# The start of a two-block network kernel: loads of parameters, input and first weights in another order, first column blocks by token halves

## The chip, the cores and the metric

The kernel runs on one core of one Trainium2 chip. The metric is the device time of one execution, in microseconds; the median of the runs counts.

## What is computed

The reference is two blocks of a sequence model on one sequence of 1024 tokens with 1024 features in float32. The first has an RWKV-7 branch and a differential attention, both fed from one projection, then a mixture of 32 experts and a gated embedding; the second has three recurrent mixers (SSD, HGRN, S5). What matters here is how the first one begins:

```python
h = rms_norm(x, norm_mix[l])
proj = h @ w_in[l]
p_rwkv = proj[..., :RWKV_COLS]
...
def rwkv7_branch(pr, mu, w0, ...):
    prev = jnp.pad(pr[:, :-1], ((0, 0), (1, 0), (0, 0)))
    xs = pr + (prev - pr) * mu
```

Every projected column of the RWKV branch (1792 of them) is mixed with the token before by a factor mu of its own.

## The kernel before

The kernel is written with a planner: the program says in its order which tiles are made from which, and the planner sets the order of the instructions on each engine and in each queue from its own estimate of times, the program's order being the preference among what is ready. Tiles live in pools; a pool that is closed gives its space to the next one on its side, and an instruction that writes the new tile waits until the old tile in that space has been used.

The input x has eight token tiles of 128 x 1024. norm_in (L2110) loads the gain of the norm on all partitions, then for each tile: the load (three buffers), in norm_tile (L183) the sum of squares on ScalarE (L189), a small operation on VectorE (L190), a power on GpSimd (L177), and the scaled tile on VectorE (L192). transpose_split (L195) then has TensorE transpose it in two batches of four (L202), ScalarE write the rounded part hi to hT (L205) and VectorE the rest lo (L206).

rwkv_proj (L290) goes through 14 blocks of 128 columns in the order RWKV_ORDER. load_w (L208) loads a block's weights of 1024 x 128 through one buffer and splits them in hi (ScalarE, L181) and lo (VectorE, L182), which have two buffers each. gemm_fm makes a block's product for 512 tokens, half the sequence, from eight groups of three products (L262 to L264), 24 in all, into one of two PSUM tiles "mm"; ScalarE (L303) and VectorE (L304) mix it with the token before, and the last token of the first half is kept in "edge" (L309). Both halves of a block are done before the next block. L303 and L304 need the parameters: setup_params (L149) loads 15 small arrays as rows of one tile "prows" (L156), TensorE transposes it (L159) and VectorE copies it to pcol (L160).

branches (L2133) calls norm_in, setup_params, rwkv_proj, then rope_tables (L626; tables for the attention's rotation, loaded, multiplied by the gains and stored) and rwkv_core (L325), which first stores zeros to two scratch arrays (L331 to L337), loads constants, and then works through eight units of the recurrence. Behind it come the attention's projections, the gates' (16 blocks) and the attention. All these loads and most stores are issued by SyncE's queue.

Of the kernel before, what the change touches and what calls it, by code (L numbers as in the profile page):

```python
# [11 lines left out]
F32 = mybir.dt.float32  # L12
F32R = mybir.dt.float32r
I32 = mybir.dt.int32
# [8 lines left out]
T = 1024  # L23
D = 1024
# [4 lines left out]
def make_consts():  # L29
    """Constants that depend on shapes alone, one column block each of a [128, n] array."""  # L30
# [57 lines left out]
def flat(ap):  # L88
    """A contiguous DRAM array as one axis."""
    n = 1  # L90
    for s in ap.shape:
        n *= s
    return bass.AP(tensor=ap.tensor, offset=ap.offset, ap=[[1, n]])
# [6 lines left out]
class Parts:  # L100
    """A weight matrix split in hi + lo, in tiles of `part` blocks of 128 rows."""
# [9 lines left out]
class Kern:  # L111
# [19 lines left out]
    def const(self, *names, pool=None):  # L131
        """Load constants to SBUF tiles."""
# [15 lines left out]
    def setup_params(self):  # L148
        nc = self.nc  # L149
        with self.pool(name="prow", bufs=1) as pool:  # L150
# [3 lines left out]
            for nme, c in PARAM_ROWS:  # L154
                self.pat[nme] = o
                nc.sync.dma_start(rows[o:o + c, :], flat(self.ap[nme]).rearrange("(r c) -> r c", c=128))  # L156
# [9 lines left out]
    def bcast_row(self, pool, src, n, name, bufs=None):  # L166
        """A DRAM vector on every partition."""
# [3 lines left out]

    def rsqrt(self, out, v):
        """out = v ** -0.5, on [128, few]."""
# [5 lines left out]
    def split(self, hi, lo, src):  # L179
        """src as the sum of two float32r parts."""  # L180
# [3 lines left out]
    def norm_tile(self, pool, x, gain, out=None):  # L184
        """rms_norm of a token tile [128, 1024]."""
# [3 lines left out]
        nc.scalar.activation(h, x, AF.Square, accum_out=st[:, 0:1])  # L189
        nc.vector.tensor_scalar(st[:, 1:2], st[:, 0:1], 1.0 / D, EPS, op0=OP.mult, op1=OP.add)  # L190
        self.rsqrt(st[:, 2:3], st[:, 1:2])
        nc.vector.scalar_tensor_tensor(h, x, st[:, 2:3], gain, op0=OP.mult, op1=OP.mult)  # L192
        return h

    def transpose_split(self, hi, lo, h, j, nk=8, k0=0, tag="t"):  # L195
        """Token tile j [128, nk*128] -> feature-major hi / lo [128, k, tokens]."""
        nc = self.nc
        for q in range(nk // 4):
# [7 lines left out]
            nc.vector.tensor_sub(lo[d], pv, hi[d].bitcast(F32))  # L206

    def load_w(self, pool, w, segs, kt=KT, raw_bufs=1, bufs=2, part=4):  # L208
        """Weight columns [kt*128, segs] -> float32r hi, lo, in tiles of `part` row blocks."""
# [5 lines left out]
        for k0 in range(0, kt, part):  # L215
            raw = pool.tile([128, part, n], F32, name=self.name("wr"), tag="wraw", bufs=raw_bufs)
            lo = pool.tile([128, part, n], F32R, name=self.name("wl"), tag="wlo", bufs=bufs)
            o = 0
            for c0, c in segs:
                nc.sync.dma_start(raw[:, :, o:o + c], wv[:, k0:k0 + part, c0:c0 + c])  # L220
                o += c
            hi = pool.tile([128, part, n], F32R, name=self.name("wh"), tag="whi", bufs=bufs)
# [5 lines left out]
    def resident_w(self, pool, w, k0, kt, cs, name, raw_bufs=2, gain=None, raws=None):  # L228
        """Row blocks k0..k0+kt-1 of w, columns cs -> Parts in one pair of tiles; a generator, a block at a time,
        that returns it. gain [128, kt]: a factor of every row; raws(k): a tile for the load of a block."""  # L230
# [17 lines left out]
    def finish(self, g):  # L248
        """What the generator g returns."""
# [9 lines left out]
    def mm3(self, out, a, b, first, last):  # L259
        """out += a^T b with a, b split in (hi, lo)."""  # L260
# [1998 lines left out]
```

## Time and profile before

| | us |
|---|---|
| median of three runs | 3081.0 |
| lowest, highest | 3079.27, 3085.3 |
| span of the profiled execution | 3076.1 |
| TensorE busy in it | 2897.0 |
| VectorE busy | 1965.6 |
| ScalarE busy | 1319.5 |

The span reaches from the first to the last instruction of the profiled execution; its time outside the span isn't recorded by itself, and the median of the runs is 4.9 us above the span. PE is TensorE's products, PEld its loading of weights, DVE is VectorE, ACT ScalarE, POOL GpSimd, SPq SyncE's queue of DMA issues. A busy TensorE isn't one at its full speed: its granted clock has two levels, 1.00 standing for 2.4 GHz and 0.50 for 1.2 GHz.

### The profile page before, as it was taken

Reading aid. Unit: us, or ns where it says so; the run is one execution under the profiler, and the core shown is the slowest. Engines: PE = TensorE matmul, PEld = TensorE weight load, DVE = VectorE, ACT = ScalarE, POOL = GpSimd, SP = SyncE. Lnnn points to the kernel's source line nnn. Section 1 sums busy time; section 2 is a strip of 40 time slices with the busy share of each in tenths; the row PEclk is TensorE's granted clock in tenths of the full one; section 3 lists DMA queues with packets and bytes.
Section 4 is the critical chain, followed back from the end, with each engine's and each line's share of the span. In section 5 each row is a group of like instructions: output and inputs, shape, how many; then the busy total and the mean of one; then the engine's idle time right before and its main releaser. Section 6 shows DMA issues by size and latency. Waiting matters only on the chain. (4 is left out here: it accounts for less than half of the span.)

```text
span 3076.1 us, 47278 instructions
## 1 busy us (share of the span) xinstructions
PE 2897.0 (94%) x18410; PEld 2400.8 (78%) x18410; DVE 1965.6 (64%) x3826; ACT 1319.5 (43%) x2167; POOL 231.9 (8%) x193
## 2 busy tenths in 40 slices
PE   6999999998998989889999997999999999999998
PEld 4888888775776867678777775878988999987776
DVE  4335778644454656679988786688546754548663
ACT  3222223213454222668777775444323343333341
POOL 0000111000000000012121110000000000000000
PEclk9999989997998998999999998999999999999999
DMA  5323333323114455799999995433344442137433
GB/s 162 115 89 82 102 116 107 101 65 106 62 62 144 152 187 195 247 339 378 370 347 335 319 346 212 138 105 95 102 129 128 133 133 74 55 106 232 125 124 127
DMA packets 378145, 503.30 MB, mean 164 GB/s; under 512 B 86039, under 2 KB 234422, under 8 KB 377918
## 3 DMA queue, kind: packets, MB, share of 16 engines
q1 hardware_dynamic: 347742, 458.63, 45.1%
q0 software_dynamic: 11296, 24.57, 2.2%
q10 hardware_dynamic: 18880, 17.05, 1.6%
q8 instruction: 146, 2.39, 0.3%
q14 instruction: 81, 0.66, 0.1%
HBM read 410.26 MB, written 106.68 MB: 168 GB/s over the span
## 5 line engine op out<-in xcount | busy, mean ns | idle before, releaser
L182 DVE TENSOR_TENSOR wh<-we,wh 128x1024 fp32r<-128x1024 f32 x384 | 452.8, 1220 | 72.3 <-ACT wh L181 70.3
L181 ACT ACTIVATE wh<-we 128x1024 fp32r<-128x1024 f32 x384 | 388.5, 1058 | 59.2 <-PE b L264 32.4
L262 PE MATMUL mm<-wh,hU 128*128 128x256 f32 (+1 forms) x768 | 253.3, 332 | 5.3 <-DVE z L1358 4.0
L263 PE MATMUL mm<-wl,hU 128*128 128x256 f32 (+1 forms) x768 | 251.8, 328 | 2.5 <-DVE wl L182 2.4
L264 PE MATMUL mm<-wh,hU 128*128 128x256 f32 (+1 forms) x768 | 250.0, 326 | 0.0
L264 PE MATMUL mm<-wh,hT 128*128 128x256 f32 (+1 forms) x640 | 215.1, 337 | 0.0
L262 PE MATMUL mm<-wh,hT 128*128 128x256 f32 (+1 forms) x640 | 207.0, 341 | 2.4 <-ACT ye L1060 2.3
L262 PE MATMUL mm<-hT,wh 128*128 128x512 f32 x480 | 196.5, 409 | 4.3 <-DVE edge L309 4.2
L182 DVE TENSOR_TENSOR wl<-wr,wh 128x1024 fp32r<-128x1024 f32 (+2 forms) x102 | 116.0, 1139 | 122.6 <-ACT wh L181 113.8
L264 PE MATMUL mm<-hT,wl 128*128 128x512 f32 x480 | 191.9, 400 | 0.0
L181 ACT ACTIVATE wh<-wr 128x1024 fp32r<-128x1024 f32 (+2 forms) x102 | 100.9, 992 | 211.3 <-PE mm L263 156.8
L263 PE MATMUL mm<-hT,wh 128*128 128x512 f32 x480 | 191.5, 399 | 0.0
L262 PEld LDWEIGHTS mm<-wh,hU 128*128 128x128 f32 x768 | 183.0, 239 | 9.6 <-DVE z L1358 5.0
L263 PEld LDWEIGHTS mm<-wl,hU 128*128 128x128 f32 x768 | 184.0, 240 | 5.8 <-DVE wl L182 3.5
L264 PEld LDWEIGHTS mm<-wh,hU 128*128 128x128 f32 x768 | 184.3, 240 | 1.4 <-issue 1.4
L262 PEld LDWEIGHTS mm<-wh,hT 128*128 128x128 f32 x640 | 125.0, 196 | 21.3 <-issue 4.3
L264 PEld LDWEIGHTS mm<-wh,hT 128*128 128x128 f32 x640 | 125.5, 196 | 12.6 <-issue 1.5
L262 PE MATMUL mm<-hU,wh 128*128 128x512 f32 x320 | 128.6, 402 | 4.5 <-ACT wh L181 4.5
L263 PE MATMUL mm<-hU,wh 128*128 128x512 f32 x320 | 127.3, 398 | 0.0
L264 PE MATMUL mm<-hU,wl 128*128 128x512 f32 x320 | 126.7, 396 | 0.0
L263 PE MATMUL mm<-wl,hT 128*128 128x256 f32 x384 | 115.8, 302 | 1.9 <-DVE wl L182 1.9
L262 PEld LDWEIGHTS mm<-hT,wh 128*128 128x128 f32 x480 | 92.3, 192 | 31.4 <-ACT xs L303 4.5
(704 smaller groups left out, 7098.1 us busy)
## 6 DMA issues: line engine op xcount, KB each, us to landing
we<-w_gate SPq DMA_DIRECT2D x64, 1024.0 KB
we<-w_up SPq DMA_DIRECT2D x64, 1024.0 KB
we<-w_down SPq DMA_DIRECT2D x64, 1024.0 KB
wr<-w_in SPq DMA_DIRECT2D x86, 512.0 KB
d_gate<-gz SPq DMA_DIRECT2D x32, 256.0 KB
gt<-d_gate SPq DMA_DIRECT2D x16, 512.0 KB
x<-d_x SPq DMA_DIRECT2D x16, 512.0 KB
dec<-sd_cum SPq DMA_DIRECT2D x16, 512.0 KB
```

Of the source, the lines that this page charges most:

```text
L181: self.nc.scalar.activation(hi, src, AF.Copy)
L182: self.nc.vector.tensor_sub(lo, src, hi.bitcast(F32))
L262: nc.tensor.matmul(out, a[0], b[0], start=first, stop=False)
L263: nc.tensor.matmul(out, a[0], b[1], start=False, stop=False)
L264: self.last = nc.tensor.matmul(out, a[1], b[0], start=False, stop=last)
```

## The change

Five things change; all lies in the first stage.

- setup_params is called ahead of norm_in, and its 15 loads are issued from ScalarE's queue.
- norm_in has eight buffers for x, in a pool on the other side of the memory, and issues all loads first: x tile 0, the gain, x tiles 1 to 3, the first block's weights, x tiles 4 and 5, the second block's weights, x tiles 6 and 7. The two weight tiles have buffers of their own in that pool.
- The split of the first block's weights stands behind the norm of tile 2, that of the second behind tile 4's.
- rwkv_proj does the first two blocks (12 and 13) by token halves: first half of both, then second half of both.
- rope_tables and the zeros (now rwkv_scratch) are queued behind the last x load on SyncE and behind the last split of the input on VectorE (issue_after adds an order on the same engine, without a wait between engines).

Lines that only lost a comment are left out here.

```diff
     def setup_params(self):
...
-                nc.sync.dma_start(rows[o:o + c, :], flat(self.ap[nme]).rearrange("(r c) -> r c", c=128))
+                nc.scalar.dma_start(rows[o:o + c, :], flat(self.ap[nme]).rearrange("(r c) -> r c", c=128))
...
+    @contextmanager
+    def issue_after(self, *instructions):
+        with ExitStack() as es:
+            for i in instructions:
+                es.enter_context(self.tc.issue_after(i.ins))
+            yield
...
-        nc.scalar.activation(h, x, AF.Square, accum_out=st[:, 0:1])
+        sq = nc.scalar.activation(h, x, AF.Square, accum_out=st[:, 0:1])
...
-        nc.vector.scalar_tensor_tensor(h, x, st[:, 2:3], gain, op0=OP.mult, op1=OP.mult)
+        self.normed = sq, nc.vector.scalar_tensor_tensor(h, x, st[:, 2:3], gain, op0=OP.mult, op1=OP.mult)
...
-            nc.vector.tensor_sub(lo[d], pv, hi[d].bitcast(F32))
+            self.last_split = nc.vector.tensor_sub(lo[d], pv, hi[d].bitcast(F32))
...
+    def load_w_steps(self, pool, w, segs, kt=KT, raw_bufs=1, bufs=2, part=4, raw_pool=None):
...
-            raw = pool.tile([128, part, n], F32, name=self.name("wr"), tag="wraw", bufs=raw_bufs)
+            raw = (raw_pool or pool).tile([128, part, n], F32, name=self.name("wr"), tag="wraw", bufs=raw_bufs)
...
+            yield
             hi = pool.tile([128, part, n], F32R, name=self.name("wh"), tag="whi", bufs=bufs)
...
-    for i in order:
-        w = K.load_w(wp, K.ap["w_in"][0], [(i * 128, 128)], part=KT)
-        mu = K.par("rwkv_mu", i)
-        edge = None
-        for hf in range(2):
+    ws = dict(zip(order, first_ws))
+    edges = {}
+    for group in (order[:2], *((i,) for i in order[2:])):
+        for hf, i in ((hf, i) for hf in range(2) for i in group):
+            if i not in ws:
+                ws[i] = K.load_w(wp, K.ap["w_in"][0], [(i * 128, 128)], part=KT)
+            w, mu = ws[i], K.par("rwkv_mu", i)
+            edge = edges.get(i)
...
+def rwkv_scratch(K, dp):
+    xds = []
+    with K.pool(name="rw_z", bufs=1, side="right") as zp:
+        zero = zp.tile([128, 1040], F32, name="rw_zero")
+        K.nc.vector.memset(zero, 0.0)
+        for i in range(2):
+            xd = dp.tile([2 * 16 * 4160], F32, name=f"rw_xd{i}", tag=f"xd{i}", bufs=1)
+            K.nc.sync.dma_start(dap(xd, 0, [[1040, 128], [1, 1040]]), zero)
+            xds.append(xd)
+    return xds
...
-def norm_in(K, x, gname, hT):
+def norm_in(K, x, gname, hT, first_w):
     nc = K.nc
-    with K.pool(name="ni", bufs=1) as pool:
+    with K.pool(name="ni", bufs=1, side="right") as pool:
+        xs = [pool.tile([128, D], F32, name=K.name("xt"), tag="xt", bufs=8) for _ in range(8)]
+        load = lambda j: nc.sync.dma_start(xs[j], x[j * 128:(j + 1) * 128, :])
+        first_ws = [first_w(i, pool) for i in range(2)]
+        load(0)
         gain = K.bcast_row(pool, K.ap[gname], D, "ni_gain")
+        for j in (1, 2, 3):
+            load(j)
+        next(first_ws[0])
+        for j in (4, 5):
+            load(j)
+        next(first_ws[1])
+        for j in (6, 7):
+            ld = load(j)
+        ws = []
         for j in range(8):
-            xt = pool.tile([128, D], F32, name=K.name("xt"), tag="xt", bufs=3)
-            nc.sync.dma_start(xt, x[j * 128:(j + 1) * 128, :])
-            K.transpose_split(hT[0], hT[1], K.norm_tile(pool, xt, gain), j)
+            K.transpose_split(hT[0], hT[1], K.norm_tile(pool, xs[j], gain), j)
+            if j in (2, 4):
+                with K.issue_after(*K.normed):
+                    ws.append(K.finish(first_ws[len(ws)]))
+    return (ld, K.last_split), ws
...
-            norm_in(K, x, "norm_mix", hT)
             K.setup_params()
-            rwkv_proj(K, hT, wp, xs_d, rp)
-            rope_tables(K, tab_d)
-            rwkv_core(K, xs_d, or_d)
+            first_w = lambda i, p: K.load_w_steps(wp, K.ap["w_in"][0], [(RWKV_ORDER[i] * 128, 128)], part=KT, raw_pool=p, raw_bufs=2)
+            after, ws = norm_in(K, x, "norm_mix", hT, first_w)
+            rwkv_proj(K, hT, wp, xs_d, rp, ws)
+            with K.issue_after(*after):
+                rope_tables(K, tab_d)
+                zeros = rwkv_scratch(K, dd)
+            rwkv_core(K, xs_d, or_d, zeros)
```

## Rows read from the trace of the kernel before

**Rows 1.** The page's busy time by engine, with share of span and instructions.

```profile
PE 2897.0 (94%) x18410; PEld 2400.8 (78%) x18410; DVE 1965.6 (64%) x3826; ACT 1319.5 (43%) x2167; POOL 231.9 (8%) x193
```

**Rows 2.** Busy time by stretch, columns in the first line.

```profile
core 0: us, PE busy (x) PEld busy (x) DVE busy (x) ACT busy (x) POOL busy (x), PEclk, DMA share, GB/s
0.00:58.60 58.60, 28.31 (x113) 21.27 (x114) 29.86 (x52) 23.58 (x39) 4.60 (x12) 0.96 0.51 165
58.60:200.00 141.40, 141.38 (x648) 112.88 (x649) 46.77 (x101) 34.92 (x50) 1.65 (x1) 0.98 0.35 111
200.00:700.00 500.00, 476.37 (x5716) 404.89 (x5716) 328.60 (x918) 137.43 (x250) 53.41 (x30) 0.95 0.34 96
700.00:800.00 100.00, 83.46 (x390) 55.25 (x386) 44.57 (x131) 37.94 (x106) 3.65 (x3) 0.76 0.26 86
```

**Rows 3.** TensorE's waits, 0 to 60 us: total, times, longest.

```profile
PE t L202 <- DVE hT L206: 11.7, 6, 3.7
PE t L202 <- DVE st L190: 10.5, 1, 10.5
PE mm L262 <- DVE edge L309: 4.2, 1, 4.2
PE t L202 <- DVE h L192: 4.0, 1, 4.0
```

**Rows 4.** The same for SyncE's queue.

```profile
SPq L156 <- DVE h L192: 13.7, 1, 13.7
```

**Rows 5.** Timeline of SyncE's queue, first and last of 15 loads (start, duration).

```profile
44.98 0.40 SPq L156 DMA_DIRECT2D prows<-rwkv_mu  x1
...
49.85 0.29 SPq L156 DMA_DIRECT2D prows<-norm_ple  x1
```

**Rows 6.** Groups by line, 0 to 58.6 us, VectorE: count, busy us, mean ns, idle before.

```profile
L206 DVE TENSOR_TENSOR hT<-t,hT 128x512 fp32r<-128x512 f32 x16 | 10.5, 680 | 4.3 <-ACT hT L205 4.3
L192 DVE SCALAR_TENSOR_TENSOR h<-xt,st,ni_gain 128x1024 f32<-128x1024 f32 x8 | 10.3, 1284 | 4.3 <-POOL st L177 4.3
...
L182 DVE TENSOR_TENSOR wl<-wr,wh 128x1024 fp32r<-128x1024 f32 x3 | 3.7, 1226 | 7.8 <-ACT wh L181 7.8
...
L304 DVE SCALAR_TENSOR_TENSOR xs<-mm,pcol,xs 128x511 f32<-128x511 f32 x2 | 1.5, 746 | 0.3 <-ACT xs L303 0.3
...
L190 DVE TENSOR_SCALAR st<-st 128x1 f32<-128x1 f32 x8 | 1.2, 148 | 7.8 <-ACT h L189 7.7
...
L639 DVE TENSOR_TENSOR da_tk_norm<-c_rope_sin,da_gk_norm 128x512 f32<-128x512 f32 x1 | 0.7, 691 | 2.3 <-DMA da_gk_norm<-k_norm 2.3
...
L309 DVE TENSOR_SCALAR edge<-mm,pcol 128x1 f32<-128x1 f32 x1 | 0.2, 210 | 0.0
```

**Rows 7.** Timeline of VectorE, the norms of the last two tiles.

```profile
40.24 1.28 DVE L192 SCALAR_TENSOR_TENSOR h<-xt,st,ni_gain 128x1024 f32<-128x1024 f32 x1 [0.73 <-POOL st L177]
...
43.67 1.28 DVE L192 SCALAR_TENSOR_TENSOR h<-xt,st,ni_gain 128x1024 f32<-128x1024 f32 x1 [0.73 <-POOL st L177]
```

**Rows 8.** Timeline of ScalarE and VectorE, first tile; idle before in brackets.

```profile
0.73 1.28 ACT L189 ACT_TABLE_LOAD   x1 [0.73 <-PEq L2248]
...
7.12 1.06 ACT L189 ACTIVATE h<-xt 128x1024 f32<-128x1024 f32 x1 [5.10 <-DMA xt<-x]
...
9.12 1.29 DVE L192 SCALAR_TENSOR_TENSOR h<-xt,st,ni_gain 128x1024 f32<-128x1024 f32 x1 [0.67 <-POOL st L177]
```

**Rows 9.** Timeline of TensorE: four transposes, and the product after its last wait.

```profile
37.06 0.60 PE L202 MATMUL t<-c_ident,h 128*128 128x128 f32 x4
...
58.62 0.77 PE L262 MATMUL mm<-hT,wh 128*128 128x512 f32 x1 [4.20 <-DVE edge L309]
```

**Rows 10.** Busy time by stretch, the 48 products from 58.62 us on.

```profile
58.62:63.40 4.78, 4.78 (x11) 3.77 (x12) 0.94 (x4) 1.02 (x2) 0.00 (x0) 0.50 0.90 265
63.80:71.90 8.10, 8.10 (x37) 6.57 (x35) 1.30 (x3) 1.32 (x2) 0.00 (x0) 1.00 0.28 98
```

**Rows 11.** Busy time by stretch, two stretches with loads; the last column is GB/s.

```profile
2.00:12.50 10.50, 1.97 (x8) 1.57 (x8) 2.87 (x5) 3.20 (x7) 1.10 (x2) 1.00 0.94 310
...
16.00:34.00 18.00, 8.10 (x29) 6.30 (x30) 11.94 (x19) 7.64 (x13) 2.20 (x4) 1.00 0.83 263
```

More of the change, by code (lines that the diff above doesn't have):

```diff
@@ L1 @@
 import math
-from contextlib import ExitStack
+from contextlib import ExitStack, contextmanager
 import numpy as np
@@ L205, in transpose_split, with load_w @@
             nc.scalar.activation(hi[d], pv, AF.Copy)
-            nc.vector.tensor_sub(lo[d], pv, hi[d].bitcast(F32))
-    def load_w(self, pool, w, segs, kt=KT, raw_bufs=1, bufs=2, part=4):
+            self.last_split = nc.vector.tensor_sub(lo[d], pv, hi[d].bitcast(F32))
+    def load_w(self, *a, **kw):
+        return self.finish(self.load_w_steps(*a, **kw))
+    def load_w_steps(self, pool, w, segs, kt=KT, raw_bufs=1, bufs=2, part=4, raw_pool=None):
         nc = self.nc
@@ L287, with rwkv_proj @@
 RWKV_ORDER = (12, 13, 4, 0, 8, 5, 1, 9, 6, 2, 10, 7, 3, 11)
-def rwkv_proj(K, hT, wp, xs_d, pool, order=RWKV_ORDER):
+def rwkv_proj(K, hT, wp, xs_d, pool, first_ws, order=RWKV_ORDER):
     nc = K.nc
@@ L307, in rwkv_proj @@
             else:
-                edge = pool.tile([128, 1], F32, name=K.name("edge"), tag="edge", bufs=2)
+                edge = edges[i] = pool.tile([128, 1], F32, name=K.name("edge"), tag="edge", bufs=2)
                 nc.vector.tensor_scalar(edge, p[:, 511:512], mu, None, op0=OP.mult)
@@ L319, with rwkv_core @@
         "y": 1, "st": 1, "ft": 1, "bon": 2}
-def rwkv_core(K, xs_d, o_d):
+def rwkv_scratch(K, dp):
[8 more added lines that the diff above has]
+    return xds
+def rwkv_core(K, xs_d, o_d, xds):
     HT = T // 2
@@ L329, in rwkv_core @@
     dp = es.enter_context(K.pool(name="rw_d", bufs=2, space=DRAM))
-    xds = []
-    with K.pool(name="rw_z", bufs=1) as zp:
-        zero = zp.tile([128, 1040], F32, name="rw_zero")
-        nc.vector.memset(zero, 0.0)
-        for i in range(2):
-            xd = dp.tile([2 * 16 * 4160], F32, name=f"rw_xd{i}", tag=f"xd{i}", bufs=1)
-            nc.sync.dma_start(dap(xd, 0, [[1040, 128], [1, 1040]]), zero)
-            xds.append(xd)
     late, mid, early = (es.enter_context(K.pool(name=f"rw_{n}", bufs=1)) for n in ("late", "mid", "early"))
```

## The prediction

> **What bounds the kernel now.** I read the profile from the coarse to the fine. The summary by engine says that TensorE works through 94% of the span [rows 1]. That is a mean over many stages, so the second view is the table of stretches [rows 2]: up to 58.6 us TensorE is busy for 28.31 us, idle for 30.3, and from 58.6 to 200 us it is busy for 141.38 of 141.40. So the kernel has a front of 58.6 us, in which something other than TensorE decides, and behind it a stretch without a hole, in which TensorE alone decides: whatever lets TensorE enter that stretch earlier moves all of it. Nothing later in this kernel depends on absolute time; later stages start when earlier ones end.
>
> The third view says what TensorE waits for in the front [rows 3]: 10.5 us until the first normed tile, 11.7 and 4.0 us between token tiles (VectorE's split of the tile before, and the norm), and 4.2 us, the last wait of all, until VectorE has used the parameters on two products (tile "edge"). All four together are 30.4 us, the whole idle time. Behind them stands SyncE's queue [rows 4]: it stood 13.7 us before the first parameter load, until VectorE's last norm gave the space free that the parameters' tile shares with the norm's. So the 15 parameter loads were issued from 44.98 to 50.14 us [rows 5], their transpose and copy came after the second product, and TensorE stood until 58.62 [rows 9].
>
> **The change, part by part.** I follow one state S through both kernels: all 64 transposes of the normed input done, 48 products (two half blocks) done, the next half block starting. Before, S is at 58.62 us [rows 9].
>
> *Parameters.* Their 15 loads, transpose, copy and what follows leave the end of the front; on TensorE that removes the last wait of 4.2 us, which is inside the difference of S below and isn't added to it. The loads come back at the very start on ScalarE's queue, ahead of its first activation. The 15 issues took SyncE 5.2 us from the first to the end of the last, 0.29 us for most and 0.40 for the longest [rows 5]. No row shows ScalarE issuing such loads; I take the same 5.2 us. Today ScalarE has loaded its table by 2.01 us and then stands 5.10 us until the first x tile has landed, at 7.12 [rows 8]. With the issues from 0.74 on and the table load of 1.28 us either ahead of or behind them, the first activation comes at 0.7 + 5.2 + 1.3 = 7.2 us, as now. So this costs nothing, hidden by the wait for x; without that cover it would cost 6 us. Bounds: at 0.40 us for each of the 15 it is 0.8 us later; if the table load falls within the loads' wait and the first x tile, which now goes ahead of the gain, lands one transfer earlier (0.5 MB at 310 GB/s [rows 11], 1.7 us), up to 1.7 us earlier. I take nothing, since this sum and today's row meet within 0.1 us.
> The Trainium skill (ScalarE: Activation LUTs, "What ACT_TABLE_LOAD costs") says that a load of 1283 ns is followed by a drain of some 1380 ns. The row here agrees with the first number; the second can't be seen, since ScalarE was waiting for x anyway. By it the first activation would be 1.4 us later and the gain so much smaller.
> The Trainium skill (DMA: Bandwidth & Descriptors, "Issuing engines are not separate DMA queues") also says that another issuing engine saves only the time of issuing, the transfers share the same engines. By it the move to ScalarE's queue is worth at most those 5.2 us of issue, and the rest comes from the new place of the parameters' tile. The rows say the same in another way: the 13.7 us were a wait for space.
>
> *x tiles and weights up front.* Ahead of the last x tile now stand the identity (64 KB), the gain, eight x tiles and two weight tiles, each 512 KB: 5.8 MB. The front moved 310 GB/s in its first full stretch and 263 in a later one [rows 11], which gives 19 to 22 us, so the last x tile lands at 21 to 25 us and the fourth at 11 to 13. The tables for the rotation, on whose loads VectorE stands today among its tiles (2.3 us ahead of one multiplication [rows 6]), wait behind the last x load (their loads) and behind the last split (their work on VectorE). What is late next is then VectorE's own work. A tile costs it a norm of 1.284 us, two splits of 0.680 and a small operation of 0.148 [rows 6]: 2.79 us. Two tiles that follow each other without other waits are 3.43 us apart, 40.24 to 43.67 [rows 7], because the small operation stands behind the splits and GpSimd's power behind it. A tile period of 2.79 and 3.43 are the bounds; I take the middle, 3.1, since with all x tiles there the squares can run ahead but the order isn't known. At 3.1 us a tile the loads are always ahead.
>
> *Token halves.* The first four tiles are enough for half a block. The first norm on VectorE starts at 9.1 us as today [rows 8]. Four tiles and one weight split of 1.226 us [rows 6]: 9.1 + 4 x 3.1 + 1.2 = 22.7 us. From there TensorE has 48 products and the other 32 transposes to do. The 48 products from 58.62 us on took 13.3 us, to 71.9, eleven of them at the granted clock of 0.50 and 37 at 1.00 [rows 10]; four transposes take 0.60 us in their midst [rows 9], so 32 take 4.8. So TensorE is done at 22.7 + 13.3 + 4.8 = 40.8 us. VectorE has in that time eight tiles, two weight splits, and the work behind two products, 2 x (0.746 + 0.210) = 1.9 us [rows 6]: 9.1 + 24.8 + 2.5 + 1.9 = 38.3 us. The later one decides: S at 40.8 us. With 2.79 us a tile it is 39.6, with 3.43 it is 42.1.
> Today the 11 products after S ran at a clock of 0.50, 4.78 us in place of 11 x 0.22 = 2.4, since TensorE had stood for 4.2 us. With TensorE at work without a pause up to S, this loss of 2.4 us lies before S, in the 13.3 us, and isn't paid again.
>
> *What moves behind.* Four table multiplications of 0.69 us [rows 6], the writing of the zeros, and their transfers (four stores of 0.5 MB and two constants) now fall at 40 to 50 us. VectorE is busy for 46.77 of 141.40 us there [rows 2] and the transfers have a share of 0.35, so they hide. What they feed belongs, in the program's order, behind all 14 blocks. If the cover were gone, the 4 x 0.69 = 2.8 us of VectorE would show. The third weight tile can load early in its old buffer; its split waits for the first block's second half, as today, and that leaves it a whole half block, 24 x 0.22 = 5.3 us [rows 10], for VectorE's 1.2 us [rows 6] and ScalarE's part ahead of it.
>
> *Sum.* 58.6 - 40.8 = 17.8 us, and 2.4 of clock: 20.2 us. Bounds: 58.6 - 42.1 = 16.5, without the clock and less 0.8 for the issues 15.7; 58.6 - 39.6 + 2.4 + 1.7 = 23.1. The profiled execution has a span of 3076.1 us; it would become 3056. The median of the three runs is 3081.0, 4.9 us more, which I take as lying around the span, unchanged. So 3081.0 - 20.2 gives 3061 us.
>
> **The rivals.** *Part is given back later.* The order of the instructions is made by a planner for the whole program, so another front can change the order of any later stage. A gap there has the size of 4.2 us [rows 3] up to the 16.5 us that TensorE stands idle between 700 and 800 us [rows 2]. With half of the larger one lost, 8 us, the time is 3069. For it speaks that such gaps exist in all later stages; against it, that the stages are shifted as a whole and keep their dependences. The same can close a gap: 3053.
> *It doesn't do what it says.* If the tiles keep the distance they have today on average, (43.67 - 9.12) / 7 = 4.9 us [rows 7, 8], because ScalarE's or VectorE's order puts the weights and the evacuations in badly, VectorE is done at 9.1 + 8 x 4.9 + 2.5 + 1.9 = 52.7 us and the gain is 6: 3075. Against it: at least the waits for the rotation's loads [rows 6] are gone, and VectorE's last two tiles kept 3.43.
> *Slower, the attention runs out of cover.* Between 700 and 800 us the granted clock is 0.76 and TensorE idles 16.5 us [rows 2]: there softmax decides, and TensorE fills up with gate blocks of 48 products, 10.9 us each at full clock (13.3 less 2.4). If the new order spends more than two of them ahead of the attention, in holes that were filled by other work, the attention stands without them. It decides from 26 us (two and a half blocks); three blocks cost 32.7 us, and the time is 3094. For it: TensorE is 95% busy from 200 to 700 us [rows 2], a block that moves forward fills little. Against it: the program's order of the gates isn't touched.
>
> **How the numbers follow.** The forecast (15.7 to 23.1 us less, 3058 to 3066) has a chance of 0.60; given back in part (3067 to 3077) 0.18, of which a tenth lies within 0.2%; a gap closed besides (3046 to 3057) 0.08; not done as said 0.08, within 0.2%; slower 0.06. About 0.2%, 6 us, is what a measurement of this kernel can tell from no change. Faster: 0.60 + 0.17 + 0.08 = 0.85; same 0.09; slower 0.06. For 8 in 10 the range takes the forecast, nearly all of the case given back and most of the gap closed: 3049 to 3075.
>
> **What would show it.** Right: in the profile after, TensorE's first product at 21 to 25 us; no wait of TensorE on "edge"; the parameters' copy before 12 us; last split of the input at 36 to 41 us; the second half of the first block starting at 39 to 42 and TensorE without a hole from there; TensorE's busy share in the first 58.6 us up by about 18 us. Wrong: the first activation later than 8 us; tiles further apart than 3.5 us on VectorE; a granted clock of 0.50 behind S; or a front that is 20 us shorter with a span that isn't, which would point at the later stages, and the stretch from 200 to 800 us would show where.

## The result, and the profile after

The changed kernel takes 3101.0 us (median of 4 runs, 3093.7 to 3101.9) where the kernel before takes 3081.6 on the same chip (4 runs). The ratio is 1.0062, with a 95% interval of 1.0045 to 1.0078: 19.4 us slower. The forecast was 3061 us, 20 us faster. The profiled execution is the fastest of the four, 3093.7 us with a span of 3091.5: some 2 us lie outside the span, not the 4.9 that the prediction took.

Busy time by stretch, the same four stretches and columns as [rows 2], kernel after:

```profile
0.00:58.60 58.60, 26.35 (x116) 20.13 (x117) 26.05 (x49) 23.00 (x39) 4.58 (x12) 0.97 0.42 136
58.60:200.00 141.40, 137.86 (x613) 110.00 (x612) 49.11 (x96) 33.95 (x48) 1.65 (x1) 0.98 0.37 117
200.00:700.00 500.00, 471.68 (x5583) 401.28 (x5581) 328.11 (x917) 134.59 (x247) 52.70 (x30) 0.93 0.34 95
700.00:800.00 100.00, 85.62 (x509) 57.51 (x509) 44.91 (x132) 37.49 (x102) 3.65 (x3) 0.78 0.29 95
```

Against [rows 2], TensorE is 1.96 us less busy in the front, where 18 more were forecast; 3.5 us less from 58.6 to 200; 4.7 us less, at a lower granted clock (0.93 for 0.95), from 200 to 700. So the loss has two places: the front, and something far behind it that the change doesn't touch.

What TensorE waits for up to 80 us, kernel after (total, times, longest), to be held against [rows 3]:

```profile
PE t L159 <- DMA prows<-norm_ple: 21.8, 1, 21.8
PE t L210 <- DVE hT L214: 8.9, 5, 3.3
PE mm L275 <- DVE xs L320: 3.5, 1, 3.5
```

The waits of 10.5, 4.0 and 4.2 us of [rows 3] are gone, the last of them, on "edge", as forecast. In their place stands one of 21.8 us at the very start, for the last parameter load, and a new one of 3.5 us behind the two blocks.

**The start.** ScalarE's timeline from 0 us (start, duration, instruction; idle before it in brackets), kernel after; it answers to [rows 5, 8]:

```profile
0.73 0.66 ACTq L156 DMA_DIRECT2D prows<-rwkv_mu  x1
...
2.07 0.32 ACTq L156 DMA_DIRECT2D prows<-rwkv_k_k  x1
3.57 0.26 ACTq L156 DMA_DIRECT2D prows<-rwkv_k_a  x1
4.37 0.26 ACTq L156 DMA_DIRECT2D prows<-rwkv_r_k  x1
...
12.42 0.25 ACTq L156 DMA_DIRECT2D prows<-hgrn_norm_w  x1
17.32 0.25 ACTq L156 DMA_DIRECT2D prows<-s_norm_w  x1
17.62 0.31 ACTq L156 DMA_DIRECT2D prows<-norm_ple  x1
17.96 1.28 ACT L197 ACT_TABLE_LOAD   x1 [17.96 <-DMA prows<-s_norm_w]
19.25 1.06 ACT L197 ACTIVATE h<-xt 128x1024 f32<-128x1024 f32 x1
```

The issues are as short as forecast, 0.23 to 0.35 us behind the first. The first four follow each other. From the fifth on there are gaps of up to 4.65 us, and the table load and the first square stand behind all fifteen: 19.25 us, for 7.12 in [rows 8]. What the gaps are, the program says. ScalarE's instructions in order, as built (numbered; in brackets the counter that is waited for):

```
4 L156 DMA prows<-rwkv_k_k 4x128
5 L156 DMA prows<-rwkv_k_a 4x128 [waits DMAHW1_49]
6 L156 DMA prows<-rwkv_r_k 4x128 [waits DMAHW3_49]
7 L156 DMA prows<-rwkv_ln_w 4x128 [waits DMAHW5_49]
8 L156 DMA prows<-rwkv_ln_b 4x128 [waits DMAHW7_49]
9 L156 DMA prows<-subln_w 1x128 [waits DMAHW1_49]
...
14 L156 DMA prows<-s_norm_w 4x128 [waits DMAHW2_49]
15 L156 DMA prows<-norm_ple 8x128 [waits DMAHW3_49]
16 L197 ACT_TABLE_LOAD
```

The program counts landed transfers on eight counters, 0 to 7, and hands them out in turn. The waits of SyncE's loads of x and weights in this stretch are on 0, 2, 4 and 6, those of ScalarE's on 1, 3, 5, 7 and again 1, 3, 5, 7: a load that comes to a used counter isn't issued until the transfer before it on that counter has landed. So ScalarE issues four loads and then stands before each further one until an earlier transfer has landed (the fifth waits for counter 1, which SyncE's identity took first). Each is small (2 KB the fourteenth), but 5 MB of x and weights are under way beside them until some 20 us: the fifth is issued 2.8 us after the first, the ninth 4.9 after the fifth. The fourteenth waits for counter 2, one of SyncE's: until SyncE's second weight tile, 512 KB issued at 11.17 us, has landed. That is the gap of 4.65 us. ScalarE works in order, so it stood for landings before it could begin to compute.

**Behind the two blocks.** VectorE's timeline from 57 us, kernel after (start, duration, line, instruction):

```profile
58.37 0.69 DVE L214 TENSOR_TENSOR hT<-t,hT 128x512 fp32r<-128x512 f32 x1 [0.16 <-ACT hT L213]
62.08 0.69 DVE L659 TENSOR_TENSOR da_tq_norm<-c_rope_cos,da_gq_norm 128x512 f32<-128x512 f32 x1 [3.02 <-DMA da_gq_norm<-q_norm]
64.42 0.69 DVE L660 TENSOR_TENSOR da_tq_norm<-c_rope_sin,da_gq_norm 128x512 f32<-128x512 f32 x1 [1.65 <-DMA da_gq_norm<-q_norm]
...
71.56 0.93 DVE L343 MEMSET rw_zero<- 128x1040 f32 x1 [3.64 <-DMA d_tab<-da_tk_norm]
72.40 1.16 DVE L190 TENSOR_TENSOR wl<-wr,wh 128x1024 fp32r<-128x1024 f32 x1
73.48 0.74 DVE L320 SCALAR_TENSOR_TENSOR xs<-mm,pcol,xs 128x511 f32<-128x511 f32 x1
```

The last split ends at 59 us. Then the work that was moved behind it stands on VectorE with its waits for transfers: 3.02 + 1.65 + 0.55 + 0.87 + 3.64 = 9.7 us idle (two of the five are in the lines left out). Behind it, in VectorE's order, wait a weight split and the evacuation of a finished block. TensorE's timeline there, kernel after:

```profile
74.27 0.50 PE L275 MATMUL mm<-hT,wh 128*128 128x512 f32 x1 [3.54 <-DVE xs L320]
...
75.58 0.63 PE L277 MATMUL mm<-hT,wl 128*128 128x512 f32 x1
76.01 0.63 PE L275 MATMUL mm<-hT,wh 128*128 128x512 f32 x1
```

TensorE has no free buffer and stands 3.54 us; from 75.6 to 79 us, at a granted clock of 0.51, its products then start 0.43 us apart in place of 0.23.

**How far behind, along the run.** For the rest I use one measure: the starts of the same SyncE instructions in two profiled executions, variant less before, as a median over 50 us. It is negative where the variant is ahead. For the changed kernel it is +3.1 us at 150 us, +4.7 at 300, +10.3 at 700, +11.9 at 1900, +15.4 at 3000. So in this execution, 15 us behind near its end, the front explains about 3.

### The profile page after: what moved, and what is told of

It reads as the page before. It is cut to its first block, busy times and chain, and to the rows that moved or that the text cites. A ratio compares the mean times of both kernels' runs of the same rounds, so it can differ in the third digit from the quotient of the medians.

```text
span 3091.5 us, 47273 instructions
## 1 busy us (share of the span) xinstructions
PE 2901.6 (94%) x18410; PEld 2405.2 (78%) x18410; DVE 1967.3 (64%) x3826; ACT 1317.0 (43%) x2167; POOL 222.4 (7%) x193
## 5 line engine op out<-in xcount | busy, mean ns | idle before, releaser
L275 PEld LDWEIGHTS mm<-wh,hT 128*128 128x128 f32 x640 | 128.2, 201 | 17.4 <-ACT ye L1081 2.7
L277 PEld LDWEIGHTS mm<-wh,hT 128*128 128x128 f32 x640 | 128.9, 201 | 14.9 <-issue 4.3
```

What stands on the lines that cost most here:

```text
L275: nc.tensor.matmul(out, a[0], b[0], start=first, stop=False)
L277: self.last = nc.tensor.matmul(out, a[1], b[0], start=False, stop=last)
```

## The experiments: the front

All times are medians, each with its ratio to the kernel before on the same chip (its medians there are 3080.2 to 3081.6).

**e1_params_sp** puts the loads back on SyncE, behind x, and keeps the rest of the change:

```diff
-                nc.scalar.dma_start(rows[o:o + c, :], ...)
+                nc.sync.dma_start(rows[o:o + c, :], ...)
...
-            K.setup_params()        # ahead of norm_in
...
+            K.setup_params()        # behind norm_in
```

> The changed kernel with the parameters undone: setup_params again stands behind norm_in, and SyncE's queue issues its 15 loads behind the last x tile; all else stays changed. Theory Q (the queue): ScalarE's 15 issues stood behind loads in flight, so that its first activation came at 19.25 us in place of 7.12, 12.1 us late; without them the first activation comes at 5.5 to 7.5 us and the third block starts about 12 us earlier than the 74.27 us of the changed kernel, at 62; if all later stages follow, the time falls from 3101 to 3089. Theory O (the order): tiles that are 4.65 us apart, since TensorE's products stand ahead of transposes, decide; then the first activation moves but the last split only by part of it. Theory P (the planner): the later stages are ordered anew and their sum moves by up to 10 us either way whatever the front does: 3079 to 3099.

Measured: 3070.9 us, 0.9961 (0.9949 to 0.9973). The front is 12.2 us ahead at 150 us, where the changed kernel is 3.1 behind. ScalarE's first lines in e1_params_sp:

```profile
0.73 1.28 ACT L197 ACT_TABLE_LOAD   x1 [0.73 <-PEq L2288]
4.77 1.06 ACT L197 ACTIVATE h<-xt 128x1024 f32<-128x1024 f32 x1 [2.75 <-DMA xt<-x]
```

With no parameter ahead, the first x tile lands 2.35 us earlier than in [rows 8]. So the 15 loads on ScalarE held its first square for 19.25 - 4.77 = 14.5 us, not for nothing.

**e2_params_pool** lets GpSimd issue them (`nc.gpsimd.dma_start`).

> The changed kernel with the 15 parameter loads issued first on GpSimd's queue in place of ScalarE's. Theory Q: ScalarE is free, first activation at 5.5 to 7.5 us; but GpSimd's power of the first tile stands behind its 15 issues of 0.55 us or more, 8 to 13 us, so the first norm on VectorE comes at 10 to 14 us in place of 21.25, and the third block 7 to 11 us earlier: 63 to 67, time 3090 to 3094 if the later stages follow. Theory P: up to 10 us to either side of that.

Measured: 3071.1 us, 0.9960 (0.9943 to 0.9976). ScalarE squares at 4.89 us, but the norm needs GpSimd's power, and GpSimd's timeline is full of issues:

```profile
10.53 0.52 POOL L156 DMA_DIRECT2D prows<-norm_ple  x1
11.16 1.09 POOL L185 TENSOR_TENSOR st<-st,mhalf 128x1 f32<-128x1 f32 x2
```

The first norm is at 11.77 us, and the front only 1.0 us ahead at 150 us. The time is the same as that of e1 although its front is 11 us worse: at 750 us e2 is 19.1 us ahead. The front doesn't explain this time either.

**e5_four_act** issues only the first four loads, those that wait for no counter, on ScalarE, and the other eleven on SyncE behind x:

```diff
-                nc.scalar.dma_start(rows[o:o + c, :], ...)
+                (nc.scalar if i < 4 else nc.sync).dma_start(rows[o:o + c, :], ...)
...
```

> The changed kernel with only the first four of the 15 parameter loads ahead on ScalarE's queue; the other eleven stand behind the last x tile on SyncE's. Loads from the two queues mark their end on eight shared counters, and an issue waits until the load before it on its counter has landed; in the changed kernel ScalarE's first four issues ran without a gap (0.73 to 2.39 us) and the fifth was the first that waited. Theory Q: with four there is no wait, the table load ends before 4 us, and the first activation starts when the first x tile lands, 4.7 to 5.5 us as in e1_params_sp; time as there, 3071, up to 8 us off by the planner's order behind the front. Rival (each issue on ScalarE costs a share of 1.15 us while large loads are in flight, 17.2 us over 15): four cost 4.6 us, the first activation comes at 6.6 us.

ScalarE's lines, e5_four_act:

```profile
2.08 0.32 ACTq L158 DMA_DIRECT2D prows<-rwkv_k_k  x1
2.43 1.28 ACT L199 ACT_TABLE_LOAD   x1 [2.43 <-issue]
4.89 1.06 ACT L199 ACTIVATE h<-xt 128x1024 f32<-128x1024 f32 x1 [1.18 <-DMA xt<-x]
```

Four issues on ScalarE are free: the first square waits for x and is within 0.12 us of e1. It is the waiting for landings that costs. The front is 13.2 us ahead at 150 us. And the time is 3111.5 us, 1.0091 (1.0070 to 1.0112), the slowest of all.

**e3_not_behind** takes away the order that puts the rotation's tables and the zeros behind the last x load and the last split (`issue_after` at line 2183).

> The changed kernel without the order that puts the rotation tables and the zeros behind the last load and the last split. Theory B (behind): VectorE's waits of 8.9 us on the loads for these (between 59 and 71.56 us) hold the evacuation of the first block's second half, TensorE waits 3.5 us on it at 74.27 and starts the third block at a lower granted clock; without the order this wait is gone, the third block starts at 70 to 71 us, and the time falls by 3.5 to 6: 3095 to 3098. Rival: the loads of the tables then fall among the x loads and cost as much: 3101.

Measured: 3099.2 us, 1.0058 (1.0038 to 1.0077). TensorE's wait there is 5.8 us, not gone: without the order they fall in the same place (the zeros at 72.77 us, for 71.56) and wait for the same transfers, 10.5 us in all for 9.7.

**e4_no_halves** does whole blocks from the start:

```diff
-    for group in (order[:2], *((i,) for i in order[2:])):
+    for group in ((i,) for i in order):
```

> The changed kernel without the token halves: each of the first two blocks is done whole, as before. Theory O: in the changed kernel 47 products of two half blocks stand among the transposes of tiles 4 to 7, which stretches the tiles to 4.65 us on average; with one half block among them the last split comes 4 to 8 us earlier, at 51 to 55 in place of 59.06, and as TensorE then still has the second block's first half to do, the third block starts at 72 to 74: no change in the time, 3099 to 3102. Theory of the forecast (halves fill TensorE's gap): the third block starts 5 us later than with the halves, 3106.

Measured: 3088.7 us, 1.0024 (1.0013 to 1.0034), with a front 3.3 us behind at 150 us, the same as with halves. **e6_sp_no_halves** is e1 and e4 together.

> The changed kernel with the parameters on SyncE's queue behind x, and without the token halves: what is left of the change is x and two weight tiles up front in own buffers, and the tables behind. Theory O (products ahead of transposes stretch the tiles): in e1_params_sp the transposes of tiles 4 to 6 stood behind products, 24.31 to 31.19 and 33.48 to 37.15 us, and the last split ended at 45.1; with one half block among the tiles it ends at 40 to 42, and since four half blocks remain the third block starts 1 to 3 us later or as early as in e1 (57 to 60). Time: without the planner 3071 to 3074; in the pair changed kernel and e4_no_halves the front moved by under 2 us and the rest by 10, so the planner may put it at 3060 to 3080. Theory of the forecast (halves fill the gap and are worth 5 us): 3076.

Measured: 3093.3 us, 1.0038 (1.0023 to 1.0053), with a front 13.7 us ahead, better than that of e1. **e8_params_space** is the kernel before with one word more, the parameters' tile on the other side of the memory, so that SyncE's wait of [rows 4] goes:

```diff
-        with self.pool(name="prow", bufs=1) as pool:
+        with self.pool(name="prow", bufs=1, side="right") as pool:
```

> The kernel before with one part alone: the parameters' tile lies on the other side of the memory, so that its loads need not wait for the norm's tiles. They are issued by SyncE behind three x tiles. Forecast's account: TensorE's last wait of the front, 4.2 us on the edge, is gone, and with it the slow clock behind it, 2.4 us: third block 4 to 6 us earlier, 3075 to 3077. Rival: 15 more issues stand ahead of x tiles 3 to 7 and of the weights, each waits for a counter, and the tiles come later by what the end gains: 3081. Theory P: up to 8 us to either side.

Measured: 3096.2 us, 1.0054 (1.0035 to 1.0072), with a front 5.0 us ahead.

Three variants have a front 5 to 14 us shorter and are 12 to 30 us slower than before. The sign of the time isn't the sign of the front. I had allowed the planner some 10 us; of my expected times for these runs only those for e3 were met to within 2 us.

## The experiments: what is behind the front

**e7_null** is the kernel before with two of its first loads swapped, the gain and the first x tile. Nothing else is touched.

```diff
-        gain = K.bcast_row(pool, K.ap[gname], D, "ni_gain")
         ...
+            if j == 0:
+                gain = K.bcast_row(pool, K.ap[gname], D, "ni_gain")
```

> The kernel before with one swap: the load of the norm's gain stands behind the load of x tile 0 in the program, nothing else. By the front alone it may start the first tile up to 1.7 us earlier, and the third block by no more: 3079 to 3082. Theory P (the planner's order of everything behind the front moves with any change of the front): the later stages differ from those of the kernel before by several us at the same front, the time lies anywhere in 3070 to 3092. Rival (the losses of the changed kernel behind its front are due to its own parts): the time is within 2 us of 3080.

Measured: 3109.2 us, 1.0082 (1.0057 to 1.0107): 28 us slower, outside the 3070 to 3092 that I had allowed. Its front is 0.4 us behind at 150 us and 0.8 at 300; at 700 us it is 27.8 behind. Busy time from 320 to 700 us, columns as in [rows 2]. Before:

```profile
320.00:700.00 380.00, 358.95 (x4401) 303.25 (x4401) 258.81 (x715) 104.22 (x190) 46.20 (x26) 0.94 0.35 100
```

e7_null:

```profile
320.00:700.00 380.00, 328.90 (x4069) 281.29 (x4070) 252.62 (x701) 96.41 (x177) 44.96 (x26) 0.89 0.32 91
```

After:

```profile
320.00:700.00 380.00, 354.90 (x4283) 300.45 (x4279) 258.80 (x713) 101.72 (x188) 45.99 (x26) 0.92 0.35 98
```

e7_null has TensorE 30 us less busy here, and at 0.89 in place of 0.94. This is the stretch of the RWKV recurrence, chains of small products with VectorE between them, which TensorE fills with blocks of the gates. Its waits from 200 to 740 us, e7_null, the two largest (total, times, longest):

```profile
PE b L576 <- DVE st L577: 14.0, 8, 5.9
PE t L410 <- ACT sq L407: 6.9, 2, 4.6
```

The same two, before:

```profile
PE b L576 <- DVE st L577: 4.9, 4, 3.3
PE t L410 <- ACT sq L407: 0.7, 2, 0.4
```

The largest after; its L431 is L410 of before:

```profile
PE t L431 <- ACT sq L428: 13.6, 4, 5.7
```

They are the recurrence's own waits, with no gate block in them. The first gate store and the recurrence's last store on SyncE's queue, before:

```profile
590.42 0.33 SPq L2129 DMA_DIRECT2D d_gate<-gz  x1
...
728.89 0.32 SPq L608 DMA_DIRECT2D d_or<-o  x1
```

e7_null:

```profile
650.80 0.32 SPq L2130 DMA_DIRECT2D d_gate<-gz  x1
...
756.69 0.32 SPq L608 DMA_DIRECT2D d_or<-o  x1
```

After, they are at 625.6 and 736.0 us. Where the gates start later, the recurrence ends later: over all 18 profiled kernels the two rise together, from 561.5 and 709.0 us (e1) to 650.8 and 756.7 (e7_null), in nearly the same order. The instructions themselves are the same; what differs is the order in which the planner issues them: between before and e7_null, as built, some 3400 of the 15,137 places of TensorE's order and 950 of VectorE's 3864 are different.

That is still a correlation. The next runs take the order itself in hand: each engine's instructions behind a point of the program are chained, one behind the other, in a given order. In outline (the order itself is a long list in the program):

```diff
+    for engine, order in ORDER:            # taken from the kernel whose order is to be kept
+        for a, b in zip(order, order[1:]):
+            tc.add_manual_dep(b, a.name, NoSync)   # issue order only, no wait
```

**e9_order_of_null**: the kernel before, with its own loads, in the order of e7_null.

> The kernel before, its loads and its front as they are; but behind the first 200 instructions of the program every engine's instructions are issued in the order that the planner made for e7_null (the kernel that differs from before by two swapped loads and took 28 us more). Theory (the loss behind the front is the planner's order, nothing else): the time of e7_null, 3109 us (3104 to 3114), and the recurrence's last store at 757 us. Rival (e7_null was slow because of the swapped loads themselves): 3081 us, as before.

Measured: 3105.1 us, 1.0081 (1.0060 to 1.0101), and from 320 to 700 us, e9_order_of_null:

```profile
320.00:700.00 380.00, 332.09 (x4138) 284.05 (x4137) 255.76 (x708) 97.21 (x179) 44.97 (x26) 0.91 0.33 93
```

As built, its TensorE order is that of e7_null in every place. The last store of the recurrence comes at 749.5 us, not quite the 757 expected. Same loads, same front, 25 us more: order alone does it, nearly all of what the swap did.

**e10, e11 and e12** go the other way: the changed kernel, e5 and e6 in the order of the kernel before, kept behind set-up and projections.

> The changed kernel with its front as it is; but behind the first two sections of the program (set-up and projections) every engine's instructions are issued in the order that they have in the kernel before. Theory (of the 19.5 us lost, 3.1 are the front's and the rest is the order): 3081.3 + 3.1 = 3084.4 us (3081 to 3089), delay against before the same at 150, 750 and 1900 us. Rival (the new front harms the later stages by itself, through clock, space or transfers): 3097 to 3103 us, as the changed kernel.

> e5_four_act (token halves and x up front, four parameter loads on ScalarE ahead, eleven on SyncE behind x; 12 to 13 us ahead of before at 150 us, yet 30 us slower at the end) with the later sections issued in the order of the kernel before. Theory: the front's gain goes through to the end, 3081.3 - 13 = 3068 us (3064 to 3073). Rival: 3111 us, as without the kept order.

> e6_sp_no_halves (parameters on SyncE behind x, whole column blocks, x and weights up front; 13.7 us ahead of before at 150 us, 12 us slower at the end) with the later sections issued in the order of the kernel before. Theory: 3081.3 - 13.7 = 3067.6 us (3064 to 3072). Rival: 3093 us, as without the kept order. It also says what the token halves are worth with nothing else moving: against e11 the difference is expected within 2 us.

Measured: e10 3098.2 us, 1.0055 (1.0035 to 1.0074): the rival's number. e11 3080.6, 0.9997 (0.9986 to 1.0007): 31 us less than e5, and still 12 above the theory. e12 3065.1, 0.9946 (0.9926 to 0.9966): as the theory has it. The delay says why two fell short. From 200 to 1900 us it changes by about 1 us in all three (e10 +13.2 and +13.9, e11 -7.4 and -6.4, e12 -14.2 and -13.0); but in e10 and e11 it jumps by 7 us between 150 and 200. The projections' 672 products were not in the chain. In e11 and e12 the last of them starts at 202.2 and 202.6 us, but up to 200 us e11 has done 50 of the recurrence's products "ra, bk", e12 64. So e10 and e11 were no clean test.

**e13 to e16** keep the order of before from the fifth column block's products on, so that TensorE's order, as built, is that of before from its 263rd instruction (of 15,137) at the latest.

> The changed kernel; behind its own front every engine issues in the order of the kernel before, now from the fifth column block's products on (e10 kept it only behind the projections). Theory: 3081 + 3 to 5 (its delay at 150 us) = 3085 us (3082 to 3089), and a delay that stays flat from 150 to 1900 us. Rival (the new front harms the later stages by itself): 3097 to 3103 us.

> e5_four_act in the order of the kernel before from the fifth column block on. Theory: 3081 - 13 = 3068 us (3065 to 3072). Rival (as e11, where 7 us were lost at 190 us although the sections behind were kept): 3078 to 3083 us.

> e1_params_sp (token halves, all 15 parameter loads on SyncE behind x) in the order of the kernel before from the fifth column block on. Theory: 3081 - 12 = 3069 us (3065 to 3073), within 2 us of e1_params_sp itself, whose own order happened to keep the front's gain. Rival (its own order was a good one, worth as much as others lost): 3075 to 3085 us.

> e6_sp_no_halves (whole column blocks, parameters on SyncE) in the order of the kernel before from the fifth column block on. Theory: 3081 - 14 = 3067 us (3063 to 3070), as e12. Token halves worth anything (forecast in the prediction): e15 at least 5 us below e16. Token halves worth nothing here: e15 0 to 4 us above e16.

Measured, with the same kernel in its own order beside it (times in us; delay against before in us at three points, same order):

| front | own order | same order, ratio (95%) | 150 | 700 | 1900 |
|---|---|---|---|---|---|
| the change | 3101.0 | e13 3090.9, 1.0027 (1.0013 to 1.0041) | +7.2 | +6.0 | +9.5 |
| four loads on ScalarE | e5 3111.5 | e14 3071.5, 0.9966 (0.9952 to 0.9980) | -10.8 | -10.5 | -10.6 |
| all on SyncE, halves | e1 3070.9 | e15 3070.6, 0.9961 (0.9947 to 0.9975) | -11.2 | -8.0 | -6.4 |
| all on SyncE, whole blocks | e6 3093.3 | e16 3065.4, 0.9951 (0.9932 to 0.9970) | -14.3 | -17.0 | -17.7 |

Now the times follow the fronts: the four delays at 150 us and the four times less 3081 (+9.8, -9.6, -10.5, -15.7) have the same order (the middle two lie within the noise) and differ by 0.7 to 2.6 us. Behind 1900 us the profiled executions drift further, to +13.4, -7.4, -1.1 and -16.5 at 3000 us; they are single executions, and e15's took 3077.0 us where its median is 3070.6. From 320 to 700 us, e13_after_same_order is back at the value of before:

```profile
320.00:700.00 380.00, 357.72 (x4336) 300.65 (x4336) 258.32 (x717) 102.98 (x189) 46.15 (x26) 0.95 0.35 99
```

e13 came out 6 us above its expectation: its delay at 150 us is +7.2 where the changed kernel has +3.1, so keeping the order lengthens this front by some 4 us. Of these, 1.8 are its wait for "xs" behind the two blocks (5.3 us for 3.5). The changed kernel's 19.4 us are then about 3 to 10 of the front and 10 to 16 of the order; the runs don't part them closer. What the loads on ScalarE cost the front shows in the same table: e13 lies 20.3 us above e15, which differs from it only in these loads and their place.

**What the halves are worth.** e15 and e16 differ in them alone. Busy time by stretch, e15_sp_halves_same_order:

```profile
35.00:40.00 5.00, 4.86 (x28) 3.83 (x26) 2.14 (x4) 2.17 (x5) 0.21 (x1) 1.00 0.00 0
40.00:45.00 5.00, 2.22 (x9) 1.55 (x9) 3.67 (x5) 1.71 (x4) 0.34 (x1) 0.73 0.00 0
45.00:50.00 5.00, 2.62 (x6) 2.15 (x7) 4.21 (x11) 2.52 (x4) 0.00 (x0) 0.50 0.31 93
```

e16_sp_whole_same_order:

```profile
35.00:40.00 5.00, 2.82 (x17) 1.88 (x17) 3.42 (x6) 2.44 (x6) 0.55 (x1) 0.92 0.00 0
40.00:45.00 5.00, 5.00 (x18) 3.81 (x18) 4.07 (x9) 1.72 (x3) 0.00 (x0) 0.74 0.17 50
45.00:50.00 5.00, 5.00 (x24) 4.14 (x23) 1.95 (x3) 1.64 (x2) 0.00 (x0) 1.00 0.99 263
```

TensorE's timeline, the last transposes, e15_sp_halves_same_order:

```profile
42.09 1.75 PE L212 MATMUL t<-c_ident,h 128*128 128x128 f32 x8 [2.23 <-DVE h L202]
...
47.38 0.76 PE L277 MATMUL mm<-hT,wh 128*128 128x512 f32 x1 [2.50 <-DVE edge L327]
```

e16_sp_whole_same_order:

```profile
38.31 1.46 PE L212 MATMUL t<-c_ident,h 128*128 128x128 f32 x8 [2.18 <-DVE hT L216]
...
46.81 0.39 PE L277 MATMUL mm<-hT,wh 128*128 128x512 f32 x1
```

The last line of each, 47.38 and 46.81 us, is the 49th product, the start of the third half block (the prediction's state S).

With halves TensorE has products to do from 21.9 us on and does them between the transposes: it has hardly a gap from 25 to 40 us. But the last transposes come 3.8 us later for it (42.09 for 38.31), and when they come, all products that were possible are done. TensorE then stands behind the last tile and the parameters, 2.5 us for "edge", and goes on at a granted clock of 0.50. Whole blocks let it idle earlier, between the transposes, and of the 48 products 24 are left to do behind them. So S comes 0.6 us later with halves, and the products behind it are slow up to 52.6 us. The halves' cost is 3.1 us in the delay and 5.2 in the medians; the intervals of the two ratios overlap, so it is shown that they aren't a gain here, not that they cost 5. In both kernels the parameters come behind x; an earlier place for their transpose, at 44.40 us in e15, wasn't tried.

## Why the prediction was wrong

The sum was 17.8 us for state S and 2.4 for the clock. S comes at 57.54 us after, for 58.62 before and 40.8 forecast. In e1, without the loads on ScalarE, it comes at 47.32: the first step below took 10.2 of the missing 16.7 us, the tiles and the halves the other 6.5. Three stretches bear on the steps (last columns: granted clock, DMA share, GB/s). Before, the 15 issues of [rows 5]:

```profile
45.00:50.20 5.20, 4.57 (x15) 3.16 (x16) 3.31 (x5) 1.20 (x2) 0.00 (x0) 0.67 0.06 14
```

After, the issues on ScalarE from the eighth on, and the products behind S:

```profile
5.00:20.00 15.00, 0.00 (x0) 0.00 (x0) 0.00 (x0) 2.03 (x2) 0.00 (x0) 1.00 1.05 362
57.54:62.50 4.96, 4.96 (x14) 3.91 (x14) 1.78 (x3) 0.60 (x1) 0.00 (x0) 0.56 0.58 167
```

By its steps:

- **Parameters "cost nothing, hidden by the wait for x"** is the step that failed first. The issues themselves were right (0.23 to 0.35 us); that fifteen of them run without a gap was wrong. I bounded the price by the length of an issue, +0.8 us, and wrote that no row shows ScalarE issuing such loads. The bound had to reach to the landing of transfers, which issues can wait for; the first activation came 12.1 us later than before and 14.5 later than in e1. I had read the price in a stretch almost without transfers (a DMA share of 0.06) and spent it in one full of them (1.05). The first x tile's earlier landing, bounded at 1.7 us, was 2.35 us (e1).
- **Up to 25 us for the last x tile**: it landed at 20, since the loads ran at 362 GB/s from 5 to 20 us, more than [rows 11].
- **A tile period of 3.1 us, bounds 2.79 and 3.43**: failed. The norms start at 21.25 and 53.80 us, seven periods of 4.65. Even with x and ScalarE free it is (40.67 - 7.15) / 7 = 4.8 in e15 and (36.37 - 7.11) / 7 = 4.2 in e16. I counted VectorE's work alone; a split waits for ScalarE's copy, that for TensorE's transposes, and these stand between products (in e15, up to 45 us, VectorE waited 8.7 us for such copies). The rival "it doesn't do what it says" had this distance nearly right (4.9) but was called unlikely (0.08).
- **Halves** as the main gain, TensorE full from 22.7 us: the first product is at 21.9 us in e15, but filling TensorE early made the transposes late. In e15, whose parameters come behind x, TensorE then waits for "edge" again (2.5 us); in the changed kernel it waits 2.94 us for the last tile.
- **2.4 us of clock**: not won. It hung on TensorE working without a pause up to S; behind those 2.94 us without work the products behind S ran at 0.56.
- **"So they hide"**, of what moves behind: failed. VectorE was free, as [rows 2] said, but it stood 9.7 us for these steps' transfers, in order ahead of an evacuation; TensorE paid 3.5 us and the slow products. I costed the work and not its waits. Undoing the order alone (e3) didn't help.
- **Later stages "are shifted as a whole and keep their dependences"**: true at a fixed order (from 200 to 1900 us the delay moves by 0.2 us in e14, 1.2 in e12, 2.3 in e13, 3.4 in e16, 4.8 in e15) and false as the kernel is built. I named the planner in a rival and priced it at 8 us; swapping two loads measured 28, and four fronts in their own order lie 0.3 to 40 us above the same fronts in the order of before.
- **The slower rival** (3094 us, 0.06) had the sign. Its mechanism wasn't seen: it wanted gate blocks to be spent too early and the attention to starve from 700 to 800 us, where TensorE is 85.62 us busy for 83.46. The gates came later, by 35 us, and the largest wait grew in the recurrence, from 0.7 to 13.6 us.

By the Trainium skill (DMA: Bandwidth & Descriptors, "Issuing engines are not separate DMA queues"), which says that another issuing engine saves only the time of issuing, I had taken 5.2 us as the most the queue could matter. The trace agrees in that the loads of both queues went through at one time (1.05 and 362 GB/s from 5 to 20 us), and adds what follows here: small loads land late beside large ones, and the engine that issues them stands. That held the first square for 14.5 us, and at the same order the move cost 20.3 us (e13 for e15). By the same skill (ScalarE: Activation LUTs, "What ACT_TABLE_LOAD costs") a drain of some 1380 ns comes on top of a table load of 1283 at every switch to another set. The load agrees, 1.28 us. The drain isn't in the trace: the first square starts at 19.25 us, 0.01 us behind the table load's end, and so does what follows ten of the fourteen table loads of the changed kernel.

**What stays open:** why the planner's order is good for some fronts (e1 in its own order equals e15; e2 gains 18 us between 150 and 750 us) and bad for others. The runs show that it is the order and where it loses, not what in the planner's reckoning turns it. e1 and e2 have the earliest gates of all (first store at 561.5 and 565.0 us), but no run moves the gates alone. A variant that beats both kernels is there twice: e16, 3065.4 us, whose order has to be written out, and e1, 3070.9 us, whose good order is luck.

## What to carry to other kernels

Loads put ahead of an in-order engine's first work cost here what they waited for, not what they took to issue: look in the program for the waits on their issues, and put no more there than are issued without one. Where a planner orders the whole program, change something that can't matter first and see how far the time moves; here that was 28 us, more than any front gave, and an effect smaller than that is known only with the order held fixed. Work that let the bottleneck engine start earlier was worth nothing here, since it went ahead of the work that the last input needed.

## What the runs showed of the hardware

- The gap between two parameter issues on ScalarE reached 4.65 us (12.67 to 17.32), for issues of 0.25 us, while SyncE's loads were landing; on GpSimd the same fifteen took 9.8 us from 1.28, 0.52 each, with two waits of 1.33 and 0.46 us.
- Behind 3.54 us without work TensorE ran its first five products 0.23 to 0.34 us apart, then eight 0.40 to 0.43, then again 0.23 (granted clock 0.97 from 74.27 to 75.58 us, 0.51 to 78.97, then 1.00): the lower clock didn't begin with the work. In e15 the stretch from 45 to 50 us, 2.4 us without work and then products, was at 0.50 throughout (the lower level, 1.2 GHz).
- A stretch with every load in flight moved 362 GB/s (5 to 20 us).
